# A list scheduler's figures for hand-overs, scratch loads and the memory path that VectorE and GpSimd share, changed in a one-core decoder kernel

## The chip, the cores and the metric

The kernel runs on one core of a Trainium2 chip. A core has five engines with a queue of instructions each: TensorE (PE) for matrix products, VectorE (DVE), ScalarE (ACT), GpSimd (POOL) and SyncE (SP), which here issues the transfers. An engine takes its instructions in the order in which they stand in its queue; between engines they wait for each other through semaphores. The time is that of the device for one execution, in microseconds (us), as a median of several runs.

## The reference

One step of a two-layer decoder trunk, for a prompt of 512 tokens and 8 samples of 8 tokens that share the weights; the model width is 1024. Layer 0 mixes tokens by pooling, layer 1 by a gated delta rule (GDN); each mixer is followed by a SwiGLU feed-forward net (FFN), with a norm before and after every block:

```
x = x + rms_norm(mixer(rms_norm(x, norm_mix_pre[i])), norm_mix_post[i])
h = rms_norm(x, norm_ffn_pre[i])
x = x + rms_norm(swiglu(h, ffn_w_in[i], ffn_w_out[i]), norm_ffn_post[i])
```

The pooling mixer takes trailing means over 2, 4, 8 and 16 positions, minus the token, then a linear map per group of channels. The GDN mixer projects to q, k, v, a gate z and two scalars per head, runs a short convolution of width 4 with SiLU over q, k and v, normalizes q and k, and then follows, per head, the recurrence

```
S_t = a_t S_{t-1} + k_t (beta_t (v_t - a_t S_{t-1}^T k_t))^T,   o_t = S_t^T q_t
```

which the reference computes in chunks of 64 tokens with a triangular solve; there are 16 heads of 128 by 128. Then `y = (rms_norm(o, o_norm) * silu(z)) @ w_out`. The outputs are the activations of both groups of tokens, the new pooling and convolution buffers, and the new states.

## The kernel before

The activations lie transposed, channels on the partitions, with the 576 tokens along the free axis. They are worked on in two halves (256 and 320 tokens around the norms and the out-projection, 288 and 288 in the FFN). Every fp32 product is made of three products of parts: an input is split into hH and hL, a weight into wh and wl, and PE forms hH·wh, hL·wh and hH·wl (`mm3`). ACT makes wh out of the loaded wraw, VectorE wl. The matmuls are named by their PSUM tiles in the profile: ps_m for the projections of GDN, ps_A and ps_B for the gate, up and out products of the FFN and the out-projection, ps_k, ps_s and ps_x for the small products and transposes in the delta rule, ps_n for the norms. The FFN's gate and up products go by Strassen's scheme.

GDN works through the 16 heads in four groups. For a group, `project` makes q, k and v, `core` builds the decay masks (des, QD), the products of k (TQ, BD, Uw) and the inverse of the triangular matrix by rows (ii, ia), and `scan` carries the state S over the chunks. `vt` and `vs` hold the prompt's and the samples' v or output, `oss` the factor of a norm that scales them. Results of a group wait in DRAM scratch tiles (og_d, z_d, gc_d, y_d) and are loaded again by `out0`, which forms the out-projection of the earlier heads while the last group is still running. `nct` and `nco` carry the new convolution buffer out.

Between the out-projection and the second FFN stands a chain: the partial sums are added (yo), their squares summed (nacc, then a product with ones on PE), a reciprocal root is computed on VectorE in eleven short steps (nv, nrc, nt), transposed on PE, multiplied in (yo<-yo,prm), added to the residual x, and the same once more for the norm ahead of the FFN.

The program doesn't call the engines itself. Each call is recorded by `Plan.put` with its possible engines, its predecessors and its cost from `Plan.cost`; some element-wise operations may go to either VectorE or GpSimd. `finish` then plans the whole program with `forward`, a list scheduler: the engine that is free first takes the ready operation of the highest rank. `LAT` is the time from an operation's end until the waiting one of another engine may start. A matmul that PE would wait for over 300 ns gets filler matmuls in front (`idle_until`; they multiply a tile of ones into a free PSUM bank, ps_w<-ones, and their result is not used). For VectorE and GpSimd `forward` keeps in `port` until when one of them holds the memory path that both use:

```
if e == "DVE" and ops[i][8] or e == "POOL" and ops[i][9] != "memset":
    other = port["POOL" if e == "DVE" else "DVE"]
    late = max(other - 130.0 - t, 0.0)
    hold, done = hold + late, done + late
```

Here `ops[i][8]` is true for an operation with no operand in PSUM that is a two-input operation, a copy or a scalar operation, and `ops[i][9]` is the method's name. The ranks come from a backward pass and are then moved by stored random numbers, `CHOSEN`, one list of seeds for each step of 30 us of the plan; they were found for the figures that stand in the planner. What `finish` issues is the order that this plan gives, so a figure of the planner is no instruction on the chip and only changes the queues' order and, for operations that may go to two engines, the engine. All operations are issued from one line, L685 in the kernel before, and the fillers from L681.

Of the kernel before, what the change touches and what calls it, by code (L numbers as in the profile page):

```python
# [60 lines left out]
class Plan:  # L61
# [11 lines left out]
    LAT = {"PE": 55.0, "ACT": 36.0, "DVE": 36.0, "POOL": 70.0, "SP": 60.0}  # L73
# [445 lines left out]
    def cost(self, eng, method, out, ins, k):  # L519

        n = self.size(out)
        if method == "dma_start":
            m = n * list(out.ap)[0][1]
            flat = len(list(out.ap)) == 2
            hold = 2500.0 if out.space == DRAM and ins[0].space == DRAM else \
                (520.0 if flat else 480.0) if m > 16384 else 460.0 if flat else 360.0
            return hold, 2000.0 + m * 4 / 240.0
# [1889 lines left out]
```

## Time and profile before

| | |
|---|---|
| median of three runs | 1490.3 us (1489.76 to 1495.96) |
| the profiled execution | 1492.77 us, span 1491.0 us |
| mean granted TensorE clock | 0.999 |
| PE busy | 1466.2 us, 98% of the span |
| VectorE busy | 1127.1 us, 76% |
| ScalarE busy | 845.7 us, 57% |
| GpSimd busy | 110.6 us, 7% |

By time the program goes through the start and the pooling mixer (to about 100 us), the first FFN (to 430), GDN with its projection (about 470 to 1025) and the rest of its out-projection (to 1078), the second FFN (to 1450) and the end. A row of the profile names an operation by its output and its inputs, with shapes of partitions by elements. In a timeline the first number is the start in us, the second the duration of the row, "x3" that three like instructions were put together; a bracket at the end gives the idle time of the engine ahead of it and what ended it. In a list of waits the numbers are the sum in us, the count and the longest. A filler, and every other matmul in plain fp32, appears as two instructions. Busy times of PE are those of pipelined matmuls, which overlap.

### The profile page before, as it was taken

What the parts mean: (1) busy time and instruction counts of PE and PEld (TensorE: products, weight loads), DVE (VectorE), ACT (ScalarE), POOL (GpSimd) and SP (SyncE); (2) the same over time, 40 slices, a digit from 0 to 9 for tenths busy, and PEclk for the clock granted to TensorE, in tenths of its full rate; (3) what the DMA queues carried; (4) which work ended last, traced back from release to release, by engine and by line L of the source; (5) the groups of instructions that cost most, each with busy time, mean ns of one, the idle gap of its engine ahead of it and who ended that gap; (6) DMA issues with size and microseconds to landing.
All of it is one profiled execution on the core that took longest, in us unless ns stands there. A gap on an engine that the chain in (4) does not pass through costs nothing.

```text
span 1491.0 us, 30006 instructions
## 1 busy us (share of the span) xinstructions
PE 1466.2 (98%) x11638; PEld 1425.8 (96%) x11638; DVE 1127.1 (76%) x2263; ACT 845.7 (57%) x1858; POOL 110.6 (7%) x255
## 2 busy tenths in 40 slices
PE   8999999999999999999999999999999999999997
PEld 7999999999999899999999899899999999999997
DVE  7994666668678698896997898567896576757855
ACT  7754443435545876765875875465574453534545
POOL 4200000000012010111020120000110000000000
PEclk9999999999999999999999999999999999999999
DMA  7543323233446334434344344747653323324263
GB/s 201 175 136 97 106 77 95 75 102 109 127 141 172 110 110 114 120 102 134 105 125 133 112 129 150 225 120 216 209 176 108 101 85 91 91 85 120 59 172 101
DMA packets 324685, 186.96 MB, mean 125 GB/s; under 512 B 13751, under 2 KB 317408, under 8 KB 324535
## 3 DMA queue, kind: packets, MB, share of 16 engines
q1 hardware_dynamic: 324543, 185.04, 42.9%
q8 instruction: 92, 1.51, 0.4%
q14 instruction: 50, 0.41, 0.1%
HBM read 154.72 MB, written 30.52 MB: 124 GB/s over the span
## 4 chain that ended last, share of the span: by engine, by line
PE 60%; issue 27%; DVE 8%; DMA 2%; ACT 2%; POOL 1%; POOLq 0%; SPq 0%; ACTq 0%; DVEq 0%
PE ps_m L685 18%; PE ps_B L685 16%; PE ps_A L685 13%; PE ps_k L685 4%; PE ps_s L685 4%; PE ps_x L685 2%; PE ps_e L685 1%; DVE ac L685 1%; DVE wl L685 1%; DMA og<-og_d 1%; DVE y L685 1%; PE ps_n L685 0%; PE ps_g L685 0%; DVE nacc L685 0%; DVE Uw L685 0%
## 5 line engine op out<-in xcount | busy, mean ns | idle before, releaser
L685 ACT ACTIVATE wh<-wraw 128x1024 fp32r<-128x1024 f32 (+4 forms) x214 | 208.2, 974 | 181.4 <-PE ps_B L685 68.8
L685 DVE TENSOR_TENSOR wl<-wraw,wh 128x1024 fp32r<-128x1024 f32 (+4 forms) x213 | 238.0, 1118 | 64.9 <-ACT wh L685 39.8
L685 PE MATMUL ps_m<-hH,wh 128*128 128x320 f32 (+1 forms) x832 | 251.2, 315 | 2.1 <-ACT zz L685 2.1
L685 PE MATMUL ps_m<-hL,wh 128*128 128x320 f32 (+1 forms) x832 | 247.0, 307 | 0.0
L685 PE MATMUL ps_m<-hH,wl 128*128 128x320 f32 (+1 forms) x832 | 244.3, 307 | 0.0
L685 PEld LDWEIGHTS ps_m<-hH,wh 128*128 128x128 f32 x832 | 154.3, 189 | 5.6 <-ACT zz L685 2.3
L685 PEld LDWEIGHTS ps_m<-hL,wh 128*128 128x128 f32 x832 | 154.8, 189 | 2.0 <-issue 0.6
L685 PEld LDWEIGHTS ps_m<-hH,wl 128*128 128x128 f32 x832 | 154.2, 189 | 1.2
L685 PE MATMUL ps_B<-hL,wh 128*128 128x288 f32 (+2 forms) x420 | 121.7, 304 | 0.4 <-POOL hL L685 0.4
L685 PE MATMUL ps_B<-hH,wl 128*128 128x288 f32 (+2 forms) x420 | 122.1, 303 | 0.0
L685 PE MATMUL ps_B<-hH,wh 128*128 128x288 f32 (+2 forms) x420 | 121.7, 304 | 0.3 <-ACT hH L685 0.3
L685 PE MATMUL ps_A<-aL,wh 128*128 128x288 f32 (+2 forms) x408 | 115.1, 296 | 0.0
L685 PE MATMUL ps_A<-aH,wl 128*128 128x288 f32 (+2 forms) x408 | 115.0, 297 | 0.0
L685 PE MATMUL ps_A<-aH,wh 128*128 128x288 f32 (+2 forms) x408 | 114.9, 297 | 0.0
L685 PE MATMUL ps_A<-hH,wh 128*128 128x288 f32 (+2 forms) x396 | 110.9, 289 | 0.7 <-DVE yo L685 0.4
L685 PE MATMUL ps_A<-hH,wl 128*128 128x288 f32 (+2 forms) x396 | 110.5, 290 | 0.4 <-DVE wl L685 0.3
L685 PE MATMUL ps_A<-hL,wh 128*128 128x288 f32 (+2 forms) x396 | 110.3, 288 | 0.0
L685 PE MATMUL ps_B<-aH,wh 128*128 128x288 f32 x296 | 84.9, 295 | 0.2 <-DVE y L685 0.2
L685 PE MATMUL ps_B<-aH,wl 128*128 128x288 f32 x296 | 84.4, 296 | 0.0
L685 PE MATMUL ps_B<-aL,wh 128*128 128x288 f32 x296 | 84.0, 295 | 0.0
L685 DVE SCALAR_TENSOR_TENSOR ac<-u,cwt,ac 128x600 f32<-128x600 f32 x96 | 80.0, 841 | 4.7 <-ACT ac L685 4.3
L685 PEld LDWEIGHTS ps_B<-hL,wh 128*128 128x128 f32 x420 | 77.4, 188 | 0.9 <-POOL hL L685 0.9
(456 smaller groups left out, 4012.4 us busy)
## 6 DMA issues: line engine op xcount, KB each, us to landing
wraw<-in_ffn_w_in_dram SPq DMA_DIRECT2D x64, 512.0 KB
wraw<-in_gdn_w_in_dram SPq DMA_DIRECT2D x53, 512.0 KB
graw<-in_ffn_w_in_dram SPq DMA_DIRECT2D x36, 512.0 KB
wraw<-in_ffn_w_out_dram SPq DMA_DIRECT2D x26, 448.0 KB
wraw<-in_gdn_w_out_dram SPq DMA_DIRECT2D x21, 512.0 KB
wraw<-in_ffn_w_out_dram SPq DMA_DIRECT2D x32, 320.0 KB
St<-in_state_gdn_rec_dram SPq DMA_DIRECT2D x32, 256.0 KB
out_dram<-St SPq DMA_DIRECT2D x32, 256.0 KB
```

The lines of the kernel that those rows point to most:

```text
L685: calls[e](*a, **k)
```

## The change

Three figures of the planner are changed: the time from an operation's end to its waiter's start on PE goes from 55 to 75 ns and on ScalarE and VectorE from 36 to 45 ns; a load from a scratch tile in DRAM takes 500 ns longer in the plan; and every GpSimd operation but a memset, its masks (affine_select) and copies too, now holds the path that it shares with VectorE, where only its tensor_tensor did. The seeds in `CHOSEN` are other ones: eight lists as before, 5944 seeds instead of 5756. The program calls the same operations; what differs is their order in the queues, the choice between VectorE and GpSimd, and the number of fillers. The new table is eleven lines longer, so the line that issues the operations is L697 now and that of the fillers L693.

```diff
-    LAT = {"PE": 55.0, "ACT": 36.0, "DVE": 36.0, "POOL": 70.0, "SP": 60.0}
+    LAT = {"PE": 75.0, "ACT": 45.0, "DVE": 45.0, "POOL": 70.0, "SP": 60.0}
...
     CHOSEN = (
-        "0: 12010 20390 45414 29223 81692 92613 98828 75481 96600 52442 97989 7909 32988 93347 10848 60178 7738 "
...
             hold = 2500.0 if out.space == DRAM and ins[0].space == DRAM else \
                 (520.0 if flat else 480.0) if m > 16384 else 460.0 if flat else 360.0
-            return hold, 2000.0 + m * 4 / 240.0
+            back = 500.0 if out.space != DRAM and ins[0].space == DRAM and hasattr(ins[0].tensor, "tag") else 0.0
+            return hold, 2000.0 + back + m * 4 / 240.0
...
                 other = port["POOL" if e == "DVE" else "DVE"]
                 late = max(other - 130.0 - t, 0.0)
                 hold, done = hold + late, done + late
-                if e == "DVE" or ops[i][9] == "tensor_tensor":
-                    port[e] = t + done
+                port[e] = t + done
```

How the queues' order differs, at the places that the prediction speaks of, is shown there row by row, before and of the change.

The counts of instructions stay nearly the same: PE has 55 filler matmuls in the program where it had 41, of them 15 between the out-projection and the second FFN, where there were none, and 36 in the first 82 us as before; VectorE has one planned operation fewer, ScalarE as many as before. At the residual adds ahead of the second FFN, which either engine may do, GpSimd does one of the second half's eight instead of three.

708 rows, old and new, of the table CHOSEN are left out of this document.

## The prediction

> **What bounds the kernel now.** I read the busy times first, then the chain that ended last, then the span cut into stretches, then what PE waited for.
>
> ```profile
> PE 1466.2 (98%) x11638; PEld 1425.8 (96%) x11638; DVE 1127.1 (76%) x2263; ACT 845.7 (57%) x1858; POOL 110.6 (7%) x255
> PE 60%; issue 27%; DVE 8%; DMA 2%; ACT 2%; POOL 1%; POOLq 0%; SPq 0%; ACTq 0%; DVEq 0%
> core 0: us, PE busy (x) PEld busy (x) DVE busy (x) ACT busy (x) POOL busy (x), PEclk, DMA share, GB/s
> 0.00:50.00 50.00, 44.80 (x323) 41.32 (x324) 39.85 (x117) 40.29 (x105) 19.93 (x76) 1.00 0.67 180
> 100.00:430.00 330.00, 330.00 (x2470) 329.44 (x2469) 218.09 (x333) 147.45 (x223) 0.00 (x0) 1.00 0.34 100
> 470.00:1025.00 555.00, 546.69 (x4727) 514.90 (x4726) 454.33 (x1098) 375.02 (x1067) 61.47 (x145) 1.00 0.46 131
> 1077.00:1102.00 25.00, 24.14 (x197) 23.37 (x197) 23.43 (x62) 16.59 (x30) 5.01 (x6) 1.00 0.71 213
> 1130.00:1450.00 320.00, 320.00 (x2404) 319.78 (x2403) 215.32 (x328) 144.27 (x219) 0.00 (x0) 1.00 0.35 101
> 1450.00:1491.00 41.00, 33.37 (x270) 32.80 (x268) 22.01 (x40) 20.76 (x41) 1.80 (x1) 0.95 0.31 95
> ```
>
> TensorE (PE) is busy for 98% of the span, and the chain runs through PE and its sequencer. The change adds and removes no matmul that computes something, so only PE's idle 1491.0 − 1466.2 = 24.8 us and the planner's filler matmuls can move. Of the idle time 5.2 us lie in the first 50 us and 7.6 in the last 41, where the order hardly changes. The two FFN stretches have none: 330.00 of 330 and 320.00 of 320. What is left is the delta-net (GDN) stretch with 555 − 546.69 = 8.3 us and the passage from the out-projection to the second FFN with 0.86. A better order can win some nine microseconds at the very most, or 0.6%.
>
> The three waits that top the list lie in GDN:
>
> ```profile
> PE ps_m L685 <- ACT zz L685: 2.1, 1, 2.1
> PE ps_k L685 <- DVE QD L685: 2.0, 4, 0.7
> PE ps_k L685 <- DVE BD L685: 1.5, 1, 1.5
> ```
>
> **The change, part by part.** The three figures cost nothing on the chip; what runs is the order that comes out of them. Their premise first: does a GpSimd mask hold VectorE?
>
> ```profile
> 10.12 0.22 DVE L685 TENSOR_TENSOR s_in<-t_le,seqm 64x64 f32<-64x64 f32 x1
> 10.19 0.86 POOL L685 TENSOR_SCALAR_AFFINE_SELECT eye<-eye 128x512 f32<-128x512 f32 x1
> 10.57 0.52 DVE L685 TENSOR_TENSOR s_st<-s_in,ident 64x64 f32<-64x64 f32 x1
> ```
>
> It does: s_st takes 0.52 us and ends at 11.09, with the mask (11.05), where its twin took 0.22. That is 0.3 us of VectorE, which in GDN has 555 − 454.33 = 100.7 us to spare. The truer figure is therefore worth something only where VectorE's queue is what PE waits for. Two such places I can name, and a third where it gets worse.
>
> *Passage to the second FFN: +3.0 us.* After the last out-projection matmul (1077.57) the norm of that half runs through VectorE, and the second half's first gate/up matmul (ps_B) starts at 1100.71. PE fills the time with 3 × 48 = 144 gate/up matmuls of the first half.
>
> ```profile
> 1077.57 0.31 PE L685 MATMUL ps_B<-hH,wl 128*128 128x320 f32 x1
> 1077.71 0.28 PE L685 MATMUL ps_A<-hH,wh 128*128 128x256 f32 x1
> 1077.83 0.28 PE L685 MATMUL ps_A<-hL,wh 128*128 128x256 f32 x1
> 1100.71 0.71 PE L685 MATMUL ps_B<-hH,wh 128*128 128x320 f32 x3 [0.31 <-ACT hH L685]
> L685 PE MATMUL ps_A<-hH,wh 128*128 128x256 f32 x48 | 13.9, 293 | 0.0
> 1085.59 0.49 DVE L685 TENSOR_TENSOR x<-x,yo 128x320 f32<-128x320 f32 x1
> 1092.45 0.49 DVE L685 TENSOR_TENSOR nacc<-nacc,nsq 128x320 f32<-128x320 f32 x1
> 1092.85 1.22 DVE L685 TENSOR_TENSOR wl<-wraw,wh 128x1024 fp32r<-128x1024 f32 x1
> 1084.84 2.82 POOL L685 TENSOR_TENSOR x<-x,yo 128x320 f32<-128x320 f32 x3 [12.66 <-DVE yo L685]
> 26.03 1.06 PE L681 MATMUL ps_w<-ones 128*128 128x128 f32 x8
> 26.92 0.60 PE L685 MATMUL ps_B<-ident,xt 128*128 128x128 f32 x4
> ```
>
> The same 144 stand in this place after the change, so whatever is added ahead of the first ps_B is added to the time. PE's order, before, just ahead of the sum over nacc with which the second norm of that half begins (x_2803 is the residual; two more ps_A follow, then the sum):
>
> ```order
> L685 MATMUL ps_n_3013<-ident,x_2803 128x128 x4
> L685 MATMUL ps_A<-hH,wh 128x256
> L685 MATMUL ps_A<-hL,wh 128x256
> L685 MATMUL ps_A<-hH,wl 128x256
> L685 MATMUL ps_A<-hH,wh 128x256
> L685 MATMUL ps_A<-hL,wh 128x256
> L685 MATMUL ps_A<-hH,wl 128x256
> L685 MATMUL ps_A<-hH,wh 128x256
> L685 MATMUL ps_A<-hL,wh 128x256
> L685 MATMUL ps_A<-hH,wl 128x256
> L685 MATMUL ps_n_3016<-ident,x_2803 64x128 x4
> ```
>
> and of the change, down to that sum (L693 issues the fillers, ps_w<-ones):
>
> ```order
> L697 MATMUL ps_n_3013<-ident,x_2803 128x128 x4
> L693 MATMUL ps_w<-ones 128x128 x7
> L697 MATMUL ps_A<-hH,wh 128x256
> L697 MATMUL ps_A<-hL,wh 128x256
> L693 MATMUL ps_w<-ones 128x128 x5
> L697 MATMUL ps_A<-hH,wh 128x256
> L697 MATMUL ps_A<-hH,wl 128x256
> L697 MATMUL ps_A<-hH,wh 128x256
> L697 MATMUL ps_A<-hL,wh 128x256
> L697 MATMUL ps_A<-hH,wl 128x256
> L697 MATMUL ps_n_2928<-ones,nacc 128x1 x3
> ```
>
> Fifteen fillers are new: these twelve, two some hundred rows earlier, and one in the out-projection. Eight trace rows (four matmuls, each twice in the trace) fill 26.03 to 26.92, so one takes 0.22 us and fifteen 3.3 us. PE must run them even where nothing is late. VectorE's part grows too: GpSimd does one of the eight residual adds instead of three, so VectorE has two more adds and one more nacc ahead of the end of the norm, 3 × 0.41 us (from 1092.45 to 1092.85) = 1.2 us. Its queue there is nearly full: 23.43 of 25. The two delays overlap, since fillers run while PE would wait. From below: fillers less the idle time that they replace, 3.3 − 0.86 = +2.4. From above: PE reaches the transposes of the first norm's result 20 matmuls later in its order (0.12 us each, 1077.71 to 1077.83: 2.4), plus 1.2, plus a share of another wl: +4. I take +3.0, nearer the fillers, which are certain.
>
> *Group 2 of the heads: −1.5 us.* PE idles 1.47 us for BD, the matrix that starts the triangular inverse.
>
> ```profile
> 643.30 3.01 POOL L685 TENSOR_TENSOR vt<-vt,oss 128x512 f32<-128x512 f32 x2 [0.47 <-DVE oss L685]
> 643.25 2.15 DVE L685 TENSOR_TENSOR vt<-vt,oss 128x512 f32<-128x512 f32 x2
> 645.41 1.45 DVE L685 TENSOR_TENSOR vs<-vs,oss 64x512 f32<-64x512 f32 x1
> 646.89 2.09 DVE L685 STREAM_TRANSPOSE ia<-ii 128x1024 f32<-128x1024 f32 x1
> 657.89 0.69 DVE L685 TENSOR_TENSOR vt<-ps_x,nk 128x512 f32<-128x512 f32 x1
> 653.36 0.33 PE L685 MATMUL ps_k<-ident,BD 128*128 128x128 f32 x1 [1.47 <-DVE BD L685]
> ```
>
> Both engines scale vt at the same time; VectorE's two take 2.15 us, where one that runs alone over the same size takes 0.69, and vs is caught too. The transpose ia and BD queue behind. VectorE's order, before (from the reciprocal of the norm oss down to BD):
>
> ```order
> L685 RECIPROCAL oss<-oss 128x20
> L685 TENSOR_TENSOR vt<-vt,oss 128x4x128 x2
> L685 TENSOR_TENSOR vs<-vs,oss 64x512
> L685 STREAM_TRANSPOSE ia<-ii 128x1024
> L685 TENSOR_TENSOR TQ<-ps_k,des 64x64
> L685 TENSOR_TENSOR ii<-ia,ii 128x31
> L685 TENSOR_TENSOR TQ<-ps_k,des 64x64
> L685 TENSOR_TENSOR ii<-ii 128x31
> L685 SCALAR_TENSOR_TENSOR ac<-u,cwt,ac 128x600
> L685 TENSOR_TENSOR ii<-ia,ii 128x30
> L685 SCALAR_TENSOR_TENSOR BD<-ps_k,bet,des 64x64
> ```
>
> and of the change:
>
> ```order
> L697 RECIPROCAL oss<-oss 128x20
> L697 COPY nct<-u 128x3
> L697 TENSOR_TENSOR vt<-vt,oss 128x4x128 x3
> L697 SCALAR_TENSOR_TENSOR Uw<-ps_k,bet,QD 128x128 x4
> L697 TENSOR_TENSOR QD<-ps_k,QD 128x2x128 x2
> L697 TENSOR_TENSOR St<-St,ps_s 128x512
> L697 SCALAR_TENSOR_TENSOR Uw<-ps_k,bet,QD 128x128 x4
> L697 TENSOR_TENSOR QD<-ps_k,QD 128x2x128 x2
> L697 TENSOR_TENSOR vs<-vs,oss 64x512
> ```
>
> Three vt are VectorE's now, one GpSimd's, and they and vs stand ahead of the Uw rows instead of just ahead of ia, which comes ten rows further down. 2.15 + 1.45 us of convoy in front of BD are gone, more than the 1.47 of idling; the Uw rows may take up the wait. From 0 to −1.47; I take all of it, −1.5.
>
> *The out-projection's loads: −1.5 us.* og comes back from DRAM scratch.
>
> ```profile
> 931.06 5.37 SPq L685 DMA_DIRECT2D out_dram<-nco  x8
> 936.52 1.30 SPq L685 DMA_DIRECT2D og<-og_d  x3
> 936.52 4.89 DMA og<-og_d
> 942.54 0.39 PE L685 MATMUL ps_m<-hH,wh 128*128 128x256 f32 x1 [2.06 <-ACT zz L685]
> ```
>
> On SP's queue eight writes of nco hold 5.37 us, the og load behind them lands 4.89 us after its issue, and PE has run dry for 2.06 us. SP's order at that place, before:
>
> ```order
> L685 DMA og<-og_d 128x576 x2
> L685 DMA St<-in_state_gdn_rec_dram 128x4x128 x2
> L685 DMA out_dram<-nco 3x128 x3
> L685 DMA out_dram<-nco 24x128
> L685 DMA out_dram<-nco 3x128
> L685 DMA out_dram<-nco 24x128 x3
> L685 DMA og<-og_d 128x576 x3
> ```
>
> and of the change:
>
> ```order
> L697 DMA og<-og_d 128x576
> L697 DMA wraw<-in_gdn_w_out_dram 128x8x128
> L697 DMA og<-og_d 128x576
> L697 DMA z_d<-zz 128x576
> L697 DMA wraw<-in_gdn_w_out_dram 128x8x128
> L697 DMA out_dram<-nco 3x128 x4
> L697 DMA out_dram<-nco 24x128 x4
> L697 DMA z_d<-zz 128x576
> L697 DMA og<-og_d 128x576 x3
> ```
>
> The nco writes and what they wait for come earlier in the change, and the two loads of St stand behind the og loads. But the pack of nco writes is still ahead of three og loads, and a store of z is between them. From 0 to −2.06; I take −1.5. [...]
>
> *The rest of GDN: −1.0 us.* Of its 8.3 us, 8.3 − 1.5 − 2.1 = 4.7 are left in small waits, the four for QD (2.0) among them. More spare time in every planned hand-over should thin them out, but another order opens new ones: from −4.7 to +3.0 (two new waits of the size of the ones just removed). I take a fifth off. *Fillers elsewhere* are one fewer: −0.2. The start and the tail: 0.
>
> Sum: +3.0 − 1.5 − 1.5 − 1.0 − 0.2 = −1.2 us. The profiled execution took 1492.77 us (span 1491.0), 2.5 above the median 1490.3; the sum is a difference between two orders, so on its own execution it gives 1491.6, and on the median **1489.1 us**.
>
> **The rivals.** *The small waits go (faster).* If more slack is what every hand-over lacked, GDN's 8.3 us go as a whole and the fillers only fill time that would be idle: 1490.3 − 8.3 − 0.2 = 1481.8. For it: the waits are many and short. Against it: fifteen certain fillers, and a planner that knew most of these waits already.
>
> *The last group comes late (slower).* In the change the transposes of the last heads' vt stand directly ahead of the out-projection's ps_A; before, fifteen rows of ps_m lie between. Their results go through one VectorE queue:
>
> ```profile
> 1021.84 0.75 DVE L685 SCALAR_TENSOR_TENSOR zz<-ps_x,prm,zz 128x512 f32<-128x512 f32 x1
> 1023.50 1.43 DVE L685 TENSOR_TENSOR hL<-zz,hH 128x256 fp32r<-128x256 f32 x4
> ```
>
> Four zz and four hL are 4 × 0.75 + 1.43 = 4.4 us. If PE reaches the first ps_A that needs these heads less than that after the last transpose, it idles for the difference, 4.4 at most, and the norm chain behind starts later by as much: 1489.1 + 4.4 = 1493.5. With GDN's rest at its upper end (+3.0 for −1.0) it would be 1497.5. Against it: earlier heads' rows can go first.
>
> *Nothing moves.* The places trade against each other within a microsecond: 1490.3, inside the forecast's case.
>
> **How the numbers follow.** A change under 0.5% (7.5 us) can't be told from none here. The terms' bounds add up to 2.4 − 1.5 − 2.1 − 4.7 − 0.2 = −6.1 and 4.0 + 0 + 0 + 3.0 − 0.2 = +6.8: 1484.2 to 1497.1. Forecast with its neighbours, 0.60 (all within 0.5%); the faster rival 0.22, of which 0.15 falls below 1482.8, where idle time that the trace hides inside overlapping matmuls may go too; the slower rival 0.18, of which 0.10 lies over 1497.8, with other late places. So faster 0.15, same 0.75, slower 0.10. Range: 1483 to 1497.
>
> **What would show it.** In the changed profile: ps_w rows at about 1075 to 1095 and the first 320-column ps_B of the second FFN 3 us later after the last out-projection matmul than the 23.1 us of now; no BD wait over 1 us in group 2; the wait of ps_m for zz near 940 under 1 us; PE idle in GDN about 4 us instead of 8.3. I am wrong if the passage grows by less than 2 us or more than 5, if GDN's idle time does not fall, or if an FFN stretch shows idle time.

## The result: slower by 0.22%, inside the range and on the other side of the forecast

| | before | after |
|---|---|---|
| median | 1490.22 us | 1494.95 us |
| lowest to highest | 1489.07 to 1495.96 | 1491.37 to 1497.21 |
| the profiled execution | 1492.77, span 1491.0 | 1496.28, span 1494.2 |

The ratio after to before is 1.0022, with a 95% interval of 1.0015 to 1.0029: 3.3 us slower, 2.2 to 4.3. The two medians lie further apart, 4.7 us, and the two means 3.5; the text goes by the ratio. The prediction said 1.2 us faster. The difference is smaller than the half per cent that was called "same", and the time lies between 1483 and 1497, but the sign is wrong. The ratios leave out one disturbed execution (2029.94 us, in the second experiment).

Three views of the profile after answer to those of before. First the busy times, and the span cut into the same stretches (the columns are those of the prediction's table):

```profile
PE 1472.4 (99%) x11666; PEld 1432.6 (96%) x11666; DVE 1128.2 (76%) x2262; ACT 843.8 (56%) x1858; POOL 115.6 (8%) x256
100.00:430.00 330.00, 330.00 (x2474) 329.81 (x2473) 218.62 (x334) 147.02 (x223) 0.00 (x0) 1.00 0.34 100
470.00:1025.00 555.00, 550.09 (x4726) 518.00 (x4725) 454.94 (x1100) 375.52 (x1070) 58.70 (x142) 0.99 0.47 132
1130.00:1450.00 320.00, 320.00 (x2411) 319.84 (x2409) 217.22 (x331) 146.09 (x223) 0.00 (x0) 1.00 0.34 98
```

The FFN stretches are full as before. PE idles 4.9 us in GDN instead of 8.3, about the 4 that were forecast, and yet the kernel is slower. PE's list of waits is a different one (engine and tile that wait, what they wait for, sum, count, longest):

```profile
PE ps_x L697 <- DVE vt L697: 2.3, 1, 2.3
PE ps_n L697 <- DVE nrc L697: 1.7, 1, 1.7
```

The waits for zz (2.1) and for BD (1.5) are gone. In their place stand one for vt, in GDN near 818 us, and one for nrc, the reciprocal root in the passage to the second FFN. PE's timeline around the passage shows what the second costs:

```profile
1077.05 0.31 PE L697 MATMUL ps_B<-hH,wl 128*128 128x320 f32 x1
...
1087.86 0.51 PE L697 MATMUL ps_n<-ident,nrc 128*128 128x128 f32 x3 [1.72 <-DVE nrc L697]
1094.24 1.73 PE L693 MATMUL ps_w<-ones 128*128 128x128 f32 x14
1096.43 0.38 PE L697 MATMUL ps_A<-hH,wh 128*128 128x256 f32 x1 [0.46 <-ACT wh L697]
1096.77 1.28 PE L693 MATMUL ps_w<-ones 128*128 128x128 f32 x10
1098.56 0.38 PE L697 MATMUL ps_A<-hH,wh 128*128 128x256 f32 x1 [0.51 <-ACT wh L697]
...
1105.89 0.31 PE L697 MATMUL ps_B<-hH,wh 128*128 128x320 f32 x1
```

From the last out-projection matmul (1077.05) to the first ps_B of the second half (1105.89) it is 28.84 us, where it was 23.14 (1077.57 to 1100.71). The passage has grown by 5.7 us, not by 3.0. VectorE's timeline after says where:

```profile
1077.30 1.42 DVE L697 TENSOR_TENSOR hL<-yo,hH 128x256 fp32r<-128x256 f32 x4
1079.04 0.75 DVE L697 TENSOR_TENSOR hL<-yo,hH 128x256 fp32r<-128x256 f32 x2
1079.71 0.48 DVE L697 TENSOR_TENSOR yo<-yo,ps_B 128x320 f32<-128x320 f32 x1
1082.50 0.16 DVE L697 TENSOR_SCALAR nv<-ps_n 128x3 f32<-128x3 f32 x1
1084.12 0.15 DVE L697 TENSOR_TENSOR nt<-nt,nrc 128x3 f32<-128x3 f32 x1
1084.70 2.23 DVE L697 TENSOR_TENSOR nt<-nt,nrc 128x3 f32<-128x3 f32 x1
1088.41 2.38 DVE L697 SCALAR_TENSOR_TENSOR yo<-yo,prm,ps_n 128x320 f32<-128x320 f32 x5 [0.36 <-PE ps_n L697]
1100.02 0.16 DVE L697 TENSOR_SCALAR nv<-ps_n 128x3 f32<-128x3 f32 x1
```

and VectorE's timeline before, those steps that the prediction did not show:

```profile
1078.14 0.48 DVE L685 TENSOR_TENSOR yo<-yo,ps_B 128x320 f32<-128x320 f32 x1
1080.76 0.16 DVE L685 TENSOR_SCALAR nv<-ps_n 128x3 f32<-128x3 f32 x1
1084.22 1.46 DVE L685 SCALAR_TENSOR_TENSOR yo<-yo,prm,ps_n 128x320 f32<-128x320 f32 x3
1093.99 0.15 DVE L685 TENSOR_SCALAR nv<-ps_n 128x3 f32<-128x3 f32 x1
```

The chain of the passage, step by step (nv opens each of the two reciprocal roots):

| from | to | before | after | more |
|---|---|---|---|---|
| last out-projection matmul | first nv | 3.19 | 5.45 | +2.26 |
| first nv | first yo<-yo,prm | 3.46 | 5.91 | +2.45 |
| first yo<-yo,prm | second nv | 9.77 | 11.61 | +1.84 |
| second nv | first ps_B | 6.72 | 5.87 | −0.85 |

In the first step six hL of the other half now stand ahead of the last sum yo (1079.71, which is 2.66 us after the matmul, where it was 0.57). In the second step an operation over three elements a partition, nt<-nt,nrc, takes 2.23 us, where the same form a moment earlier took 0.15. GpSimd's timeline names what ran meanwhile:

```profile
1084.53 2.38 POOL L697 TENSOR_TENSOR wl<-wraw,wh 128x1024 fp32r<-128x1024 f32 x1 [8.28 <-ACT wh L697]
```

This wl begins 0.17 us ahead of the nt, and the nt ends 0.02 us after it. So the nt was held until the wl was done: 2.23 us for 0.15. Where the wl went to VectorE, in the second experiment, the nt of this root take 0.15 to 0.16 us each. The third step holds the residual adds and squares that came to VectorE.

Near 818 us the chain of work of the kernel after shows the other new wait (start, duration, what):

```profile
812.90 5.83 DMA vt<-z_d
818.82 0.76 DVE vt L697
```

The windows of the same place show the granted clock (the last three numbers are clock, DMA share, GB/s):

```profile
815.00:820.00 5.00, 2.67 (x42) 2.34 (x42) 1.18 (x2) 2.89 (x7) 0.00 (x0) 0.96 0.74 204
820.00:825.00 5.00, 5.00 (x43) 4.21 (x42) 1.46 (x2) 0.62 (x2) 0.00 (x0) 0.50 0.39 108
825.00:830.00 5.00, 5.00 (x34) 4.39 (x37) 1.33 (x3) 2.67 (x9) 0.52 (x1) 0.86 0.53 157
```

A load of z lands 5.83 us after its issue, VectorE works it into vt (0.76 us), and PE, which has idled for 2.33 us, goes on at half the clock for 6.8 us: (0.04 + 0.50 + 0.14) × 5 us × 2.

### The profile page after: what moved, and what is told of

The parts are those of the page before. It is cut to its first block, busy times and chain, and to the rows that moved or that the text cites. A ratio compares the mean times of both kernels' runs of the same rounds, so it can differ in the third digit from the quotient of the medians.

```text
span 1494.2 us, 30061 instructions
## 1 busy us (share of the span) xinstructions
PE 1472.4 (99%) x11666; PEld 1432.6 (96%) x11666; DVE 1128.2 (76%) x2262; ACT 843.8 (56%) x1858; POOL 115.6 (8%) x256
## 4 chain that ended last, share of the span: by engine, by line
PE 88%; DVE 6%; ACT 2%; POOL 1%; issue 1%; DMA 1%; DVEq 0%; SPq 0%; POOLq 0%; ACTq 0%
PE ps_B L697 28%; PE ps_A L697 27%; PE ps_m L697 20%; PE ps_s L697 5%; PE ps_k L697 4%; PE ps_x L697 2%; DVE wl L697 1%; PE ps_e L697 1%; PE ps_n L697 1%; DVE ac L697 1%; DVE y L697 1%; DVE nacc L697 1%; PE ps_g L697 1%; ACT wh L697 0%; DMA vt<-z_d 0%
## 5 line engine op out<-in xcount | busy, mean ns | idle before, releaser
L697 ACT ACTIVATE wh<-wraw 128x1024 fp32r<-128x1024 f32 (+4 forms) x214 | 207.5, 973 | 157.1 <-PE ps_A L697 61.7
L697 DVE TENSOR_TENSOR wl<-wraw,wh 128x1024 fp32r<-128x1024 f32 (+4 forms) x213 | 238.1, 1119 | 65.8 <-ACT wh L697 50.7
L697 PE MATMUL ps_m<-hH,wh 128*128 128x320 f32 (+1 forms) x832 | 244.9, 311 | 0.3 <-ACT u L697 0.3
L697 PE MATMUL ps_m<-hH,wl 128*128 128x320 f32 (+1 forms) x832 | 243.8, 309 | 0.0
L697 PE MATMUL ps_m<-hL,wh 128*128 128x320 f32 (+1 forms) x832 | 243.7, 308 | 0.0
L697 PEld LDWEIGHTS ps_m<-hH,wh 128*128 128x128 f32 x832 | 154.1, 190 | 3.6 <-ACT u L697 1.0
L697 PEld LDWEIGHTS ps_m<-hL,wh 128*128 128x128 f32 x832 | 154.1, 190 | 2.2 <-issue 0.8
L697 PEld LDWEIGHTS ps_m<-hH,wl 128*128 128x128 f32 x832 | 153.7, 190 | 2.6 <-issue 1.2
L697 PE MATMUL ps_B<-hL,wh 128*128 128x288 f32 (+2 forms) x420 | 122.8, 304 | 0.3 <-POOL hL L697 0.2
L697 PE MATMUL ps_B<-hH,wh 128*128 128x288 f32 (+2 forms) x420 | 122.2, 304 | 0.4 <-DVE yo L697 0.4
L697 PE MATMUL ps_B<-hH,wl 128*128 128x288 f32 (+2 forms) x420 | 122.1, 303 | 0.0
L697 PE MATMUL ps_A<-aL,wh 128*128 128x288 f32 (+2 forms) x408 | 116.3, 297 | 0.0
L697 PE MATMUL ps_A<-aH,wh 128*128 128x288 f32 (+2 forms) x408 | 116.0, 297 | 0.0
L697 PE MATMUL ps_A<-aH,wl 128*128 128x288 f32 (+2 forms) x408 | 115.9, 296 | 0.0
L697 PE MATMUL ps_A<-hH,wh 128*128 128x288 f32 (+2 forms) x396 | 110.3, 290 | 1.4 <-ACT wh L697 1.0
L697 PE MATMUL ps_A<-hH,wl 128*128 128x288 f32 (+2 forms) x396 | 110.2, 289 | 0.3 <-DVE wl L697 0.3
L697 PE MATMUL ps_A<-hL,wh 128*128 128x288 f32 (+2 forms) x396 | 109.8, 289 | 0.0
L697 PE MATMUL ps_B<-aH,wh 128*128 128x288 f32 x296 | 83.9, 295 | 0.0
L697 PE MATMUL ps_B<-aL,wh 128*128 128x288 f32 x296 | 83.3, 294 | 0.0
L697 PE MATMUL ps_B<-aH,wl 128*128 128x288 f32 x296 | 83.1, 295 | 0.1
L697 DVE SCALAR_TENSOR_TENSOR ac<-u,cwt,ac 128x600 f32<-128x600 f32 x96 | 79.7, 837 | 3.8 <-ACT ac L697 3.5
L697 PEld LDWEIGHTS ps_B<-hL,wh 128*128 128x128 f32 x420 | 77.6, 188 | 0.8 <-POOL hL L697 0.8
```

What stands on the lines that cost most here:

```text
L697: calls[e](*a, **k)
```

## The experiments

The first theory was the prediction's own: the fillers of the passage cost what they take, 3.3 us. Beside it stood others, numbered as in the expectations: GpSimd's wl holds the chain (theory 2); the late vt and the half clock behind it cost the time (theory 3); the change wins in GDN and loses in the passage (theory 4), with two rivals, that GDN's order wins nothing and that the second FFN is handed over late by what runs ahead of it; the change's order is a little better everywhere but in the passage (theory 5). The sixth concerned the change as a whole, its figures against its drawn seeds. Numbers such as 11591 are positions in the list of recorded operations; `seq` is the planned order as pairs of operation and engine, a pair without an engine is a filler. Edits are made to it after planning, so nothing else moves.

### Without the fillers of the passage

```diff
+ seq = [x for p, x in enumerate(seq) if x[1] is not None or p < first]   # first: where the passage begins
```

> The changed kernel without the 15 fillers between the out-projection and the second FFN. Theory 1 (the prediction's): the fillers are PE time that the passage pays, so the first 320-column ps_B comes about 3.3 us earlier than in the changed kernel (28.8 us after the last out-projection matmul becomes 25.5) and the time falls by about 3. Theory 2: what follows the fillers waits for ScalarE's wh in any case (waits of 0.46 and 0.51 us stand right behind the two packs in the changed kernel), so PE idles where the fillers stood: 28.8 us stay within 0.5, the time stays within 0.1%, unless the granted clock drops for want of the fillers.

Measured: 1497.73 us, ratio to before 1.0047 (1.0032 to 1.0062), so slower than the change itself. PE's timeline, then the windows of the same place:

```profile
1073.91 0.31 PE L700 MATMUL ps_B<-hH,wl 128*128 128x320 f32 x1
...
1093.29 0.39 PE L700 MATMUL ps_A<-hH,wh 128*128 128x256 f32 x1 [2.03 <-ACT wh L700]
1095.42 0.58 PE L700 MATMUL ps_A<-hH,wh 128*128 128x256 f32 x1 [1.62 <-ACT wh L700]
...
1105.44 0.31 PE L700 MATMUL ps_B<-hH,wh 128*128 128x320 f32 x1
```

```profile
1090.00:1095.00 5.00, 1.76 (x13) 1.31 (x12) 5.00 (x12) 4.09 (x8) 0.00 (x0) 0.95 0.14 52
1095.00:1100.00 5.00, 4.58 (x21) 4.58 (x22) 3.97 (x10) 2.21 (x4) 0.00 (x0) 0.50 0.49 137
1100.00:1105.00 5.00, 5.00 (x40) 4.87 (x39) 2.30 (x12) 1.19 (x3) 0.00 (x0) 0.87 0.82 257
```

Where the twelve fillers stood, PE waits 3.65 us for two wh of ScalarE; with them it ran fillers for 1.73 + 1.28 us and waited 0.97, together 3.98. The fillers fill a wait that is there anyway. Without them the clock falls to half for 6.8 us, which is 3.4 us of lost work, and 1.0047 − 1.0022 is 3.7 us; the mean clock of its four executions was 0.994 to 0.997. The passage is longer for it, 31.53 us instead of 28.84; less the 3.4 it would be about 28.1, not the 25.5 of the first theory. The theory of the costly fillers falls.

### GpSimd's weight part to VectorE

```diff
+ seq[seq.index((11591, "POOL"))] = (11591, "DVE")   # the wl at 1084.53
```

> The changed kernel with one operation moved: the wl that GpSimd makes in the passage (2.38 us from 1084.53) is made by VectorE, at the same place of the plan, between the first and the second yo<-yo,prm. Theory 2 (GpSimd's wl holds VectorE's nt<-nt,nrc for 2.23 us instead of 0.16): the root chain shortens by 2.07 us, the wl costs VectorE 1.13 us behind it, PE's wait of 1.7 us for nrc goes; the first ps_B comes 0.9 us earlier, at least, and up to 2 where the wl hides. Rival: VectorE was not what PE waited for, no change within 0.3 us.

Measured: 1493.87 us, 1.0015 (1.0005 to 1.0024). PE's timeline:

```profile
1075.54 0.31 PE L699 MATMUL ps_B<-hH,wl 128*128 128x320 f32 x1
...
1103.70 0.31 PE L699 MATMUL ps_B<-hH,wh 128*128 128x320 f32 x1
```

The passage takes 28.16 us, 0.68 less, and the wait for nrc is gone. That is less than the 0.9 us expected at the least, and far less than the 2.07 us of the hold; VectorE now has the wl itself, 1.2 us of its full queue, which would leave 0.87. By the time alone this kernel is not told apart from the change, whose interval overlaps.

### Two cures for the late vt

The first moves twelve matmuls of the projection (ps_m) ahead of the four transposes that wait for vt, the second puts ten fillers there (bank and k name a free PSUM bank; the lines that find it are left out here):

```diff
+ up = [(i, "PE") for i in (8950, 8983, 8984, 8951, 8985, 8952, 8953, 8986, 8954, 8987, 8988, 8955)]
+ seq = [x for x in seq if x not in up]; p = seq.index((8716, "PE")); seq[p:p] = up
```

```diff
+ p = seq.index((8716, "PE")); seq[p:p] = [((bank, k), None)] * 10
```

> The changed kernel with twelve projection matmuls (ps_m, six of 256 and six of 320 columns, 1.6 us) moved from just behind to just ahead of the four transposes of vt that wait 2.33 us for VectorE at 817.3. Theory 3 (the idle PE makes the granted clock fall to 0.5 for 6.83 us right behind the wait): wait under 1 us, no stretch at half clock, time 1.6 + 3.4 = 5.0 us less than the changed kernel, about 1488.5. Rival (the stretch of small matmuls ahead of the wait lowers the clock, whatever waits): the wait falls by 1.6 us, the half-clock stretch stays, time 1.6 less.

> The changed kernel with ten fillers (10 x 0.22 = 2.2 us) put ahead of the same four transposes. No useful work moves, and VectorE comes no earlier. Theory 3: the wait is covered, the clock stays at 1.0, time 3.4 us less than the changed kernel. Rival: the clock falls all the same, no change within 0.3 us; if fillers only delay, 0.2 us more.

Measured: with the matmuls moved 1493.87 us, 1.0020 (1.0010 to 1.0029); with the fillers 1494.74, 1.0031 (1.0019 to 1.0044). PE's timeline with the matmuls moved, its timeline with the fillers, and the window behind the fillers:

```profile
820.05 0.66 PE L702 MATMUL ps_x<-ident,vt 128*128 128x128 f32 x4 [0.36 <-DVE vt L702]
```

```profile
817.51 2.50 PE L703 MATMUL ps_w<-ones 128*128 128x128 f32 x20
```

```profile
820.00:825.00 5.00, 5.00 (x61) 4.50 (x58) 0.71 (x2) 2.21 (x6) 0.00 (x0) 1.00 0.62 168
```

Both do at the place what was expected: the wait shrinks from 2.33 to 0.36 us, or is covered, and the half clock is not there. With the fillers the window shows 1.00; with the matmuls moved the four transposes behind the wait take 0.66 us, where in the profile of the change, at a clock of 0.50, they took 1.12. Neither makes the kernel measurably faster than the change; the 5.0 and 3.4 us that were expected did not come. In the first, new waits opened behind it (0.69 for Uw, and 1.5 at a later vt). In the second no such wait was found. Either the half clock is not in every execution of the change, or what it costs is caught up; the repetition of the change decides.

### The change once more

The kernel after, unchanged, for a second profile.

> The changed kernel itself, on the same chip as the other three, for another look at it. [...] The time is 0.2% over the kernel before.

Measured: 1494.6 us, 1.0025 (1.0014 to 1.0036). PE's timeline, and the window of GDN:

```profile
819.78 0.65 PE L697 MATMUL ps_x<-ident,vt 128*128 128x128 f32 x4 [2.14 <-DVE vt L697]
...
1074.16 0.31 PE L697 MATMUL ps_B<-hH,wl 128*128 128x320 f32 x1
1102.99 0.31 PE L697 MATMUL ps_B<-hH,wh 128*128 128x320 f32 x1
```

```profile
470.00:1025.00 555.00, 550.00 (x4752) 518.46 (x4751) 457.02 (x1106) 376.64 (x1072) 57.28 (x142) 1.00 0.47 133
```

The wait for vt is there again, 2.14 us, but the clock stays at 1.00 behind it (1.00 from 815 to 820 us and from 820 to 825), and the out-projection ends at 1074.16 instead of 1077.05. So the half clock does not belong to the order alone; it hits one execution and not another. Its price is 3.4 us of lost work by the windows. The 2.9 us between the two ends are near to that, but one pair doesn't show it: two executions of the old order, both with a clock of 1.00 in the window of GDN, end the out-projection 3.7 us apart (1077.57, and 1073.86 in the second cross below). The passage is 28.83 us again, to 0.01.

### Crosses of the two orders

If the two plans are cut in the middle of the out-projection's first half, where nearly the same operations lie behind them (all but two of 11,100), each half can be run with the other. The kernel issues such an order from a stored list.

```diff
- seq = planned order
+ seq = stored list: the first 11,100 operations in the one order, the others in the other
```

The first cross has GDN of the change and the passage of before, the second the reverse.

> A cross of the two orders: everything up to the middle of the out-projection's first half stands in the changed kernel's order (and on its engines), everything behind it in that of the kernel before. Theory 4 (the change wins in GDN and loses in the passage to the second FFN): up to the out-projection's end it is as fast as the changed kernel, 3.7 us ahead of the kernel before where the clock doesn't fall, 0.7 where it falls once; the passage takes 23 to 24 us as before; the time is 1 to 4 us less than the kernel before. Rival (each order only fits itself, or GDN's gain was one of the profiled execution alone): same as before or slower.

> The other cross: up to the middle of the out-projection's first half in the order of the kernel before, then in that of the changed kernel. Theory 4: GDN as in the kernel before, the passage takes about 28.8 us instead of 23.1, some 2 us of it come back at the second FFN's start and end (0.8 and 1.2); the time is 3 to 4 us more than the kernel before. Rival (the passage is long only because the changed order of GDN and of the out-projection hands it over late): passage near 24 to 25 us, time within 1.5 us of the kernel before.

Measured: the change's GDN with the old passage takes 1490.23 us, 0.9993 (0.9984 to 1.0003), and in five more rounds 1489.93, 0.9995 (0.9985 to 1.0005):

> The first cross once more (the changed kernel up to the middle of the out-projection's first half, then the kernel before), with more rounds, since 0.9993 could not be told from 1. Theory 4 as first held (GDN wins 3.7 us): 0.9975 to 0.999. Rival (what the profile of the kernel before lost at og was one execution's, so the two orders of GDN are worth the same): 0.9993 to 1.0003, and PE's waits for vt and for xn in GDN and at the start take what the others give.

The old GDN with the change's passage takes 1495.27, 1.0030 (1.0020 to 1.0041). PE's timeline of the first cross, and that of the second:

```profile
1074.84 0.31 PE L1315 MATMUL ps_B<-hH,wl 128*128 128x320 f32 x1
...
1098.00 0.41 PE L1315 MATMUL ps_B<-hH,wh 128*128 128x320 f32 x1 [0.31 <-ACT hH L1315]
```

```profile
1073.86 0.31 PE L1316 MATMUL ps_B<-hH,wl 128*128 128x320 f32 x1
...
1102.69 0.31 PE L1316 MATMUL ps_B<-hH,wh 128*128 128x320 f32 x1
```

The passage is 23.16 us with the old order behind the change's GDN and 28.83 with the change's order behind the old one. It does not depend on what runs ahead of it, so the theory of a late hand-over falls, and the loss lies in the part from the out-projection on: 0.30% of 1490.8 is 4.5 us. The rest of the change gives 0.05 to 0.07% back, 0.7 to 1.0 us, which is not told apart from nothing; the 1 to 4 us that were expected for it did not come.

The second cross also shows the old GDN in another execution. PE's waits for BD and zz in it, the og load in the chain of work, and the window of GDN:

```profile
PE ps_k L1316 <- DVE BD L1316: 1.5, 1, 1.5
...
PE ps_m L1316 <- ACT zz L1316: 0.4, 1, 0.4
```

```profile
934.25 3.23 DMA og<-og_d
```

```profile
470.00:1025.00 555.00, 549.79 (x4759) 518.54 (x4758) 456.87 (x1103) 377.54 (x1072) 62.37 (x145) 1.00 0.46 133
```

PE idles 555 − 549.79 = 5.2 us in it, not 8.3; the og load lands after 3.23 us, not 4.89, and the wait for zz is 0.4, not 2.1. The wait for BD is the same, 1.5.

### Giving VectorE's work in the passage back

The wl on VectorE as above, and two of the residual adds back to GpSimd, to make three, as before:

```diff
+ seq[seq.index((11591, "POOL"))] = (11591, "DVE")
+ for i in (11432, 11439): seq[seq.index((i, "DVE"))] = (i, "POOL")
```

> The changed kernel with the passage's element-wise work split between VectorE and GpSimd as in the kernel before: the wl of GpSimd goes to VectorE, and the first and the third of the eight residual adds go to GpSimd (three there again). Theory 2: with the wl alone moved the passage took 28.2 us instead of 28.8; two adds of 0.41 us fewer on VectorE make it 27.3 or 27.4, time 1.5 us less than the changed kernel. Rival (the adds are not on the path, since PE and ScalarE are late by themselves): 28.2 as with the wl alone.

Measured: 1492.46 us, 1.0011 (0.9999 to 1.0024). PE's timeline:

```profile
1074.71 0.31 PE L701 MATMUL ps_B<-hH,wl 128*128 128x320 f32 x1
...
1102.05 0.36 PE L701 MATMUL ps_B<-hH,wh 128*128 128x320 f32 x1
```

The passage takes 27.34 us: 0.68 from the wl, 0.82 from the two adds, against 2 × 0.41. The kernel is 2.1 us below the change in the same rounds, though the two intervals overlap. Of the 5.7 us, 1.5 are settled in this way. In the first step nothing has moved: in VectorE's timeline the first nv still comes 5.44 us after the last out-projection matmul, 2.25 more than before.

### The ends of the change around the middle of before

The order of the change up to about 465 us and from about 1110 us on, the order of before between.

```diff
+ seq = stored list: operations up to 4,500 and from 11,900 in the change's order, the others in that of before
```

> A third cross: the changed kernel's order at the two ends, up to the first heads' projection (about 465 us) and from behind the passage (about 1110 us) on, and the order of the kernel before between, with GDN and the passage. Theory 5 (the change's order is a little better everywhere but in the passage, most surely at the ends: 0.9 us ahead by 449 us, 1.4 to 2 us won back behind the passage): time 2 us less than the kernel before, ratio 0.9985, and less than both kernels. Rival: what was won at the ends belonged to single executions, ratio 1.000 within 0.0007.

Measured over five rounds: 1488.81 us, 0.9983 (0.9974 to 0.9992). PE's timeline gives a passage of 23.17 us, and a wait for nco in GDN that the same order met with 0.62 us in the second cross:

```profile
935.07 0.33 PE L1315 MATMUL ps_x<-ident,vt 128*128 128x128 f32 x1 [2.28 <-ACT nco L1315]
...
1073.28 0.31 PE L1315 MATMUL ps_B<-hH,wl 128*128 128x320 f32 x1
1096.45 0.41 PE L1315 MATMUL ps_B<-hH,wh 128*128 128x320 f32 x1 [0.31 <-ACT hH L1315]
```

This version is faster than both kernels, by 0.17% than before: some 2.5 us (1.2 to 3.9), although this profile has the stall for nco of 2.28 us and some 3.4 us at half the clock behind it (0.66 from 935 to 940 us). Where the 2.5 us arise is open. From the first ps_B of the passage to the last matmul it is 1479.13 − 1096.45 = 382.7 us, as before (1482.99 − 1100.71 = 382.3), which speaks for the start. But the first cross has the very same order up to GDN and wins only 0.7 to 1.0, and the traces don't bear the start out. PE reaches the transposes of a norm just ahead of GDN (ps_n<-ident,nrc) at 446.33 and 446.23 us with the old start, at 446.10 and 445.86 in the two profiles of the change, at 446.72 and 446.08 in those of the first cross, and at 444.24 here. So some 2 us of the lead in this profile belong to the execution and not to the order. That the change's GDN loses what its start wins would fit the times too, and no run shows it.

### The figures without new seeds

One figure alone, the memory path, and all three, both with the seeds of before:

```diff
-                if e == "DVE" or ops[i][9] == "tensor_tensor":
-                    port[e] = t + done
+                port[e] = t + done
```

> One figure alone: the kernel before, with GpSimd's masks and copies holding VectorE's path in the plan, and the seeds of the kernel before. Theory 6 (the stored seeds suit only the plan they were found for): the order comes out worse almost everywhere, with 113 fillers instead of 41, and the time is 20 us or more over the kernel before. Rival (the figure is what matters and the seeds only refine): within 5 us of the kernel before or faster.

> All three figures of the change with the seeds of the kernel before. Theory 6: again far slower than either kernel, by 20 us or more, with 182 fillers; what the change measures is then the new figures with their own seeds as one, and no figure has an effect that could be told apart from the draw. Rival: within 5 us of the changed kernel.

Measured, one execution each: 1552.97 and 1565.6 us, 62 and 75 us above before. The planner puts in 113 and 182 fillers, where the kernel before has 41 and the change 55. With these figures changed the old seeds no longer fit the plan for which they were drawn. The effect of truer figures can't be measured apart from the draw in this way. The hand-over and the scratch load were not tried alone.

## Why the prediction was wrong

Two steps failed: the price of the passage, and the gain in GDN, which was read from one execution. The crosses share the miss out. For the passage and what follows they measure 4.5 us (3.0 to 6.1) where the terms said +3.0; for what is ahead of it −0.7 to −1.0 where the three GDN terms and the fillers elsewhere said −4.2, which lies outside both intervals. So 1.5 us of the miss lie in the passage and 3.2 to 3.5 in GDN. With GDN alone put right the sum is already +2.0 to +2.3; with the passage alone put right it is +0.3. The sign was lost mainly in GDN.

*Passage, +3.0.* The place and the direction were right, and the fillers run where they were forecast, up to 1098 us. The size was not: +5.7 in the chain, and of this 4.0 to 4.8 are left at the end. From the first ps_B to the last matmul it is 382.3 us before, and 380.6 and 381.4 in the two profiles after, so 0.9 to 1.7 us come back in the second FFN. Three points of the working:

- "nearer the fillers, which are certain" was the wrong end to choose. The twelve fillers cost 0.3 us where they stand (3.98 against 3.65): without them PE waits for wh nearly as long, and the clock falls to 0.50 for 6.8 us. They were a sign of the wait for which the planner put them in, not its price.
- The three VectorE operations were priced at 1.2 us, and that fits: two adds given back brought 0.82; the nacc was not tried.
- VectorE's queue was counted by what was added, not by what stands ahead of the chain. The hL ahead of the last yo sum (+2.26 in that step) have no term. The wl that GpSimd takes over has no term for what it holds: the hold that the prediction had measured at the start of the program (0.52 us for 0.22) stood here in the middle of the reciprocal root, at 2.23 for 0.15. The changed figure for masks does not bear on it, since a tensor_tensor was in the plan's path before too. The upper bound of +4 was therefore too low, and "wrong if the passage grows by more than 5" came true.

That the loss lies in the order from the out-projection on is shown by the crosses. Inside it, the share of the wl and the adds was tried, 1.5 of the 5.7 us; the hL of the first step were read from the traces and not tried by a run of their own.

*Group 2, −1.5.* The wait for BD is gone, as forecast. In all three profiles with the old GDN it stands at 1.5, so this term was read from something stable. What its removal alone is worth in time was not measured.

*The og loads, −1.5.* The wait for zz is gone, but the price came from one execution: with the same order it was 0.4 us in another. The load landed 3.23 us after its issue there, and 4.89 in the one on which the prediction relied; neither one alone is the cost of this load.

*The rest of GDN, −1.0.* PE's idle time in GDN fell, but by less than one pair of profiles shows. It is 8.3, 5.2 and 6.3 in three executions of the old order (before, the second cross, the kernel with the two ends), 4.9 and 5.0 in two of the change and 5.4 in both profiles of the first cross. The means are 6.6 and 5.2, so the change is worth some 1.4 us of idle time here and not the 4 that were forecast: of the 8.3 that the prediction shared out, about 1.7 belonged to the one execution. And the waits that went were in part replaced: the vt load, issued 0.47 us behind a weight load, makes PE wait 2.3 and 2.1 us in the two profiles of the change. It was not in the sum; the range "to +3.0, two new waits" had room for it. The intervals of the crosses, for GDN and the start together, go from −2.4 to +0.7.

*The start and the tail, 0.* The cross with both ends of the change is 2.5 us faster than before, so the term may have been too high; how much of it is the order's stays open, as said above.

*The rivals.* "The last group comes late" named the right side with another cause: the hand-over into the out-projection isn't late, since its end is at 1074.2 to 1077.1 after and at 1073.3 to 1077.6 with the old GDN. "The small waits go" did not happen.

The measured parts add up: 4.5 for the passage and what follows, less 0.7 to 1.0 for what is ahead of it, makes 3.5 to 3.8, against 3.3 and 3.7 measured for the whole, which is well within their intervals.

## What to carry to other kernels

Where a plan puts fillers, it says that PE waits there; look up what PE waits for and price that, since the fillers themselves were nearly free here (3.98 us with them against 3.65), and without them the clock fell to 0.50 for 6.8 us. In a serial chain of tiny operations ask which long operation of another engine can fall between them, and price it with its whole length: here an nt of 0.15 us took 2.23 beside a wl of 2.38. And take a wait's price, and a stretch's idle time, from more than one execution before you count their removal as a gain: here 1.7 of 2.1 us for one wait were luck.

## What the runs showed of the hardware

The clock fell to half behind single waits of 2.33 us (for vt, 6.83 us at 0.50 in the profile of the change) and 2.28 us (for nco, some 3.4 us in the kernel with the two ends), and around two of 2.03 and 1.62 us close together (6.8 us, without the fillers). It did not fall behind the wait for vt of 2.14 us in the repetition of the change. In the second profile of the first cross, whose longest wait is 1.9 us, the clock is 0.75 from 820 to 825 us, and 0.96 from 430 to 470 us, where PE idles 0.65 us in all. So the length of the wait alone does not decide, and no run shows what does.

A VectorE operation over three elements a partition took 2.23 us beside a GpSimd operation of 2.38, where the same form took 0.15 a moment earlier; the chain behind it waited, PE for 1.72 us.

The same load of og took 4.89 us from issue to landing in one execution (before) and 3.23 in another of the same order (the second cross).

The time outside the span is 1.74 us before and 2.08 after in the mean, and within about 0.1 us of that in each of their runs. These 0.34 us are a tenth of the loss, and no run here says what they are. They go with the kernel: 2.07 to 2.09 in four that were edited from the change, but 1.72 where only the wl went to VectorE, so a third of what that run seemed to gain lies outside the span.
